# Layer 0's modulation by halves of the features on TensorE, with one strict order of loads

## The chip, the cores and the metric

The kernel runs on one core of a Trainium2 chip. The metric is device time in microseconds (us): the time of one execution of the whole program, of which the profile's span, from the first to the last recorded instruction, is nearly all. The core has a matrix engine (TensorE; PE in the profile, its weight loads PEld), a vector engine (VectorE, DVE), a scalar engine (ScalarE, ACT), a general engine (GpSimd, POOL) and one that only issues transfers and waits (SyncE, SP). Each engine works through its own queue in order. Sixteen DMA engines carry the transfers.

## What is computed

A backbone of two layers over 1024 latent tokens and 256 context tokens with 1024 features. Each layer normalises its tokens, scales and shifts them by a modulation that is worked out from a conditioning vector, and mixes them. Cut to what matters here (layer 0):

```python
def modulation(cond, w, b):
    m = jax.nn.silu(cond) @ w + b
    return jnp.split(m, 3, axis=-1)          # shift, scale, gate

sh_l, sc_l, g_l = modulation(c, mod_w[i], mod_b[i])
sh_c, sc_c, g_c = modulation(c_ctx, mod_w[i], mod_b[i])
h_lat = rms_norm(x_lat, norm_g[i]) * (1.0 + sc_l[:, None, :]) + sh_l[:, None, :]
h_ctx = rms_norm(x_ctx, norm_g[i]) * (1.0 + sc_c) + sh_c
y_lat, y_ctx = even_mixer(h_lat, h_ctx, ev_w_in[j], ...)   # starts with h @ w_in
```

The even mixer projects h to queries, keys, values and gates and runs two kinds of attention (global, and banded with a sink). Layer 1 runs a convolution module and a neighbourhood attention. Everything is float32; a large matmul is made of three with operands split into a high and a low part (`mm3`, L318).

## The kernel before, in words

**Layout.** Tokens lie in the free dimension, features on the 128 partitions: 1024 features are DK = 8 slices called dk. Tokens come in three chunks (`CHUNKS`): chunk 0 is the context (256 tokens), chunks 1 and 2 are 512 latent tokens each. The normalised and modulated tokens are kept as a high and a low part, h[c][0] and h[c][1], of type float32r.

**The modulation.** It has three parts (0 shift, 1 scale, 2 gate) of 1024 features, each worked out in two halves j of 512 features; one half needs 2.1 MB of `mod_w`, in four loads of 512 KB. `mod_half` (L170) does a half on TensorE: eight matmuls (L179) of the two conditioning vectors with 128 x 512 weights, a copy of the row on ScalarE (L181), four small transposes (L184), then the bias on VectorE (L188) and for the scale one more step (L190). `mod_half_v` (L194) does a half on VectorE: per dk and vector one multiply-add of 128 x 512 (L215, L220), then eight small matmuls (L226). The weights' tiles come from a ring (`mw_tile`, L150; `MWR` has six places, two of them in a pool of their own, the others in memory that the attention uses later for keys and values: tags KA, KB, V).

**The start of layer 0** (L623 to 691) is driven by the string `PLAN = 'p0mvnbwmm1h2nbhnbh'`: `0`, `1`, `2` load a chunk (`load_x`), `m` and `v` do the next modulation half on TensorE or VectorE in the order (0,0), (0,1), (1,0), (1,1) (part, j), `n` sums a chunk's squares (`norm_x`, L650), `b` turns that into the reciprocal root, spread over the partitions by small matmuls (`rstd_steps`, L245), `h` makes a chunk's h (`make_h`, L302) and `w` loads and splits the first unit's weights (`load_w0`: eight slices of 128 x 384, 192 KB each, raw tiles `wr` with WRB = 2 buffers). So (0,1) is on VectorE. `make_h` takes, per slice, one VectorE step x * scale * rstd (L307), then either ScalarE's shift into the high part and a VectorE step for the low part (L310, L311), or ScalarE's shift, ScalarE's cast (L297) and a subtraction on POOL (L300). `HV` says which.

**What sets the order.** The code gives priorities; a scheduler orders each engine's queue by a simulated timeline when the program is built, so instructions traced later can come earlier. Two means bind it. `tc.issue_after(ins)` puts the instructions of a block that run on the engine of `ins` behind it in that engine's queue; before, `after_mod(k)` puts the loads of `1`, `2` and `w` behind the last four modulation loads traced ahead of them. `later(n)` lowers priority.

**What comes after.** `proj_qkv` (L760) projects the ten blocks of 128 tokens of a unit of 384 columns: per block eight dk times `mm3`, 24 matmuls of 128 x 384, into a PSUM bank, which ScalarE copies (L773); rotary steps on VectorE and transposes (`qk_tail`) follow, and the results go to DRAM. `proj_gate` (L738) projects the gates. `fill0(0, w0)` (L836) runs this for the first unit (u = 2, as `ORDER` says) before attention starts. While it runs (`solo`), banks of tag "pp" alternate between "pp" and "mx", two buffers each (L104), and every third dk calls `tick()` (L710), which takes one step of `mods`: the remaining eight halves of modulation (layer 0's gate and layer 1), on VectorE at low priority, in tiles of the ring "ABAV" (KA, KB, KA, V). After that `attn_gen` weaves attention groups with the other units' projections; a group starts with a load of keys into a KA tile (`load_ka`, L520).

Of the kernel before, what the change touches and what calls it, by code (L numbers as in the profile page):

```python
# [18 lines left out]
P = 128  # L19
DK = 8  # L20
# [29 lines left out]
PFB = 2  # L50
MWB, WRB = 2, 2
OHQ = 0
# [17 lines left out]
GL = 12  # L70
HV = (('gggvvvvg',) * 3, ('gggvvvvg', 'vvvgvvvg', 'gggvvvvg'))
O1 = (6, 65, 41, 14)
TICK0, TICK1 = (1, 3)
PLAN = 'p0mvnbwmm1h2nbhnbh'
MWR = "ABxAVx"
XA = 4
ORDER = (2, 3, 0, 1)
# [11 lines left out]
def tile_kernel(ctx: ExitStack, tc: tile.TileContext, a, out):  # L89
# [57 lines left out]

    mm0 = []

    def mw_tile():  # L150
# [19 lines left out]
    def mod_half(pool, l, part, j):  # L170

        pb = bank("pp", nm("pm"))
        c0 = part * 1024 + j * 512
        for d2 in range(4):
            w2 = mw_tile()
            mm0.append(SY.dma_start(w2, a["mod_w"][l, 2 * d2 * P : (2 * d2 + 2) * P, c0 : c0 + 512].rearrange("(d p) n -> p d n", d=2)))
            for d in range(2):
                dk = 2 * d2 + d
                PE.matmul(pb[0:2, :], csil[:, dk, :], w2[:, d, :], start=(dk == 0), stop=(dk == DK - 1))  # L179
        row = a0.tile([P, 512], F32, tag="ost", name=nm("mrow"), bufs=2)[0:2, :]  # L180
        SC.copy(row, pb[0:2, :])  # L181
        tr = bank("tr", nm("trm"))
        for i in range(4):
            PE.transpose(tr[:, 2 * i : 2 * i + 2], row[:, i * P : (i + 1) * P], ident[0:2, 0:2])  # L184
        trv = tr[:, 0:8].rearrange("p (i c) -> p i c", c=2)
        o = part * 8 + j * 4
        dst = modT[l][:, o : o + 4, :]
        VE.tensor_tensor(dst, trv, modb[:, l, o : o + 4, None].broadcast_to([P, 4, 2]), op=ALU.add)  # L188
        if part == 1:
            VE.scalar_tensor_tensor(gs[l][:, j * 4 : j * 4 + 4, :], dst, 1.0,  # L190
                                    normg[:, l, j * 4 : j * 4 + 4, None].broadcast_to([P, 4, 2]),
                                    op0=ALU.add, op1=ALU.mult)

    def mod_half_v(pool, l, part, j, conds):  # L194

        c0 = part * 1024 + j * 512
        pool, tag, bufs = (kvp, "QH", 3) if mwp[0] is not None else (pool, "macc", 2)
        accs = [pool.tile([P, 512], F32, tag=tag, name=nm("macc"), bufs=bufs) for _ in conds]
        pre = []
        for dk in range(DK):  # L200
            if solo[0] and dk % 2 == 0:
                w2 = mw_tile()
                d_ = SY.dma_start(w2, a["mod_w"][l, dk * P : (dk + 2) * P, c0 : c0 + 512].rearrange("(d p) n -> p d n", d=2))
                if mwp[0] is not None:
                    mm0.append(d_)
                pre = [w2[:, 0, :], w2[:, 1, :]]
# [28 lines left out]
    def newton_rsqrt(pool, v, n, tag):  # L235
# [7 lines left out]
        return r  # L243

    def rstd_steps(pool, accs, n, tag, inv=1.0, tr="tr"):  # L245
# [12 lines left out]
        yield  # L258
        yield
        bc = bank(tag, nm("bc"))  # L260
        for b in range(nb):
            PE.matmul(bc[:, b * P : (b + 1) * P], r[:, b : b + 1].broadcast_to([P, P]), ident, start=True, stop=True)
        return bc
# [54 lines left out]
    def mm3(o, lh, ll, rh, rl, first, last):  # L318
        PE.matmul(o, lh, rh, start=first, stop=False)  # L319
        PE.matmul(o, lh, rl, start=False, stop=False)  # L320
        done[0] = PE.matmul(o, ll, rh, start=False, stop=last)  # L321

    raws = []

    def load_w(pool, src, c0, nco, width, bufs, leng=lambda dk: "g", dks=range(DK), rb=WPR):

        wh, wl = {}, {}
        for dk in dks:
            raw = pool.tile([P, width], F32, tag="wr", name=nm("wr"), bufs=rb)
            raws.append(SY.dma_start(raw[:, :nco], src[dk * P : (dk + 1) * P, c0 : c0 + nco]))  # L330
            h = pool.tile([P, width], F32R, tag="wh", name=nm("wh"), bufs=bufs)
# [291 lines left out]
    with ExitStack() as p0x:  # L623
        w0p = p0x.enter_context(tc.tile_pool(name="w0p", bufs=1, reuse_waits="tile"))
        W0B = 8

        def load_w0(src, u, n):
            return load_w(w0p, a[src], u * n, n, 384, W0B, rb=WRB)

        with tc.tile_pool(name="st0", bufs=1, reuse_waits="tile") as st0:  # L630
# [4 lines left out]
            def load_x(c):  # L635
# [4 lines left out]
                else:  # L640
                    t = st0.tile([P, DK, n], F32, tag=f"xr{c}", name=f"xr{c}")
                    xraw[c] = [t[:, dk, :] for dk in range(DK)]
                    for d in range(0, DK, 4):
                        SY.dma_start(t[:, d : d + 4, :],
                                     a["cT"][:, d : d + 4, :] if c == 0 else a["xT"][:, d : d + 4, 0:n])
                    return
                for dk in range(DK):
                    SY.dma_start(xraw[c][dk], a["xT"][:, dk, t0 - 256 : t0 - 256 + n])

            def norm_x(c):  # L650
                n = CHUNKS[c][1]
                acc = kvp.tile([P, 512], F32, tag="QH", name=nm("acc"), bufs=3)
                for dk in range(DK):
                    if dk == 0:
                        SC.activation(acc[:, :n], xraw[c][0], AF.Square)
                    else:
                        sq = kvp.tile([P, 512], F32, tag="QL", name=nm("sq"), bufs=3)
                        SC.activation(sq[:, :n], xraw[c][dk], AF.Square)
                        VE.tensor_tensor(acc[:, :n], acc[:, :n], sq[:, :n], op=ALU.add)
                return acc  # L660

            def norm_bc(c, acc):
                n = CHUNKS[c][1]
                return run(rstd_steps(st0, [acc], n, "st"))[:, :n]

            made = [0]
            accs, bcs, mh = [], [], [(0, 0), (0, 1), (1, 0), (1, 1)]
            mwp[0] = st0
            for ev in PLAN:
                if ev in "012":  # L670
                    with after_mod(XA):
                        load_x(int(ev))
                elif ev == "p":
                    SC.dma_start(modb, a["mod_b"])
                    SC.dma_start(normg, a["norm_g"])
                elif ev == "n":
                    accs.append(norm_x(len(accs)))
                elif ev == "w":
                    with after_mod(XA):
                        w0 = load_w0("ev_qkv", ORDER[0], 384)  # L680
                elif ev == "m":
                    mod_half(st0, 0, *mh.pop(0))
                elif ev == "v":
                    run(mod_half_v(st0, 0, *mh.pop(0), (0, 1)))
                elif ev == "b":
                    bcs.append(norm_bc(len(bcs), accs[len(bcs)]))
                elif ev == "h":
                    make_h(0, made[0], lambda dk, c=made[0]: xraw[c][dk], bcs[made[0]], h[made[0]])
                    made[0] += 1

# [904 lines left out]
```

## Time and profile before

| what | value |
|---|---|
| median of three runs | 1595.64 us (1587.97 to 1596.81) |
| the profiled execution | 1590.95 us, span 1589.2 us |
| busy: PE, DVE, POOL, ACT | 1459.0 (92%), 1124.1 (71%), 831.3 (52%), 756.6 (48%) us |
| the chain that ended last, by engine | PE 61%, DVE 15%, DMA 13%, issue 4%, POOL 3%, SPq 2% |
| bytes read from and written to HBM | 160.49 MB, 60.03 MB |

How to read it: busy time is the sum of an engine's instructions, and a busy PE is not PE at its peak, since its matmuls overlap. The profile gives, for stretches of the span, each engine's busy time, the TensorE clock that was granted (1.00 is full speed), the mean busy share of the DMA engines and the bytes moved per time. A timeline row has start, duration, engine, source line, operation, output tile, input tiles and count; square brackets hold the idle time of that engine just before, and what ended it. Line numbers are those of the kernel before; a line can be that of a helper (L300 and L297 are `split`, L319 to L321 `mm3`).

### The profile page before, as it was taken

How to read it: one execution, taken by the hardware profiler on the slowest of the kernel's cores; microseconds unless marked ns; L12 is line 12 of the kernel's file. 1: busy time of each engine (PE TensorE's matmuls, PEld its weight loads, DVE VectorE, ACT ScalarE, POOL GpSimd, SP SyncE). 2: the span in 40 equal slices, each digit the busy share in tenths (PEclk: the TensorE clock that was granted, in tenths of full speed). 3: DMA queues.
4: the chain of work that ended last, by engine and by line, in shares of the span. 5: the costliest groups of instructions: out<-in, count | busy, mean ns of one | idle time of the engine just before them, and what ended most of it. 6: DMA issues, size and time to landing. Idle time of an engine off the chain costs nothing.

```text
span 1589.2 us, 22236 instructions
## 1 busy us (share of the span) xinstructions
PE 1459.0 (92%) x6984; PEld 1180.6 (74%) x6984; DVE 1124.1 (71%) x2172; ACT 756.6 (48%) x1542; POOL 831.3 (52%) x760
## 2 busy tenths in 40 slices
PE   6789989998999988989999889999999999789895
PEld 1779867787778667767887768888887787577685
DVE  4898787588857668455478776999846467576676
ACT  2722353444434664654555564443433455545473
POOL 1561364455636667756654655754532334444575
PEclk9999999998999999989999989999999999799997
DMA  9548234532442123471111122213456878888732
GB/s 316 179 144 270 83 101 138 176 95 80 146 143 75 36 65 113 156 223 51 57 40 44 57 66 79 92 55 107 162 176 219 246 222 262 239 219 232 221 97 106
DMA packets 198462, 222.01 MB, mean 140 GB/s; under 512 B 18812, under 2 KB 154696, under 8 KB 198344
## 3 DMA queue, kind: packets, MB, share of 16 engines
q1 hardware_dynamic: 191680, 209.02, 42.9%
q10 hardware_dynamic: 6664, 11.57, 2.4%
q8 instruction: 55, 0.90, 0.2%
q14 instruction: 63, 0.52, 0.1%
HBM read 160.49 MB, written 60.03 MB: 139 GB/s over the span
## 4 chain that ended last, share of the span: by engine, by line
PE 61%; DVE 15%; DMA 13%; issue 4%; POOL 3%; SPq 2%; ACT 1%; DVEq 0%; POOLq 0%; ACTq 0%
PE p L320 6%; PE p L319 6%; PE p L321 6%; PE ov L411 4%; PE ov L413 4%; PE ov L412 3%; PE po L320 3%; PE po L319 3%; PE po L321 3%; PE st L448 3%; PE st L452 3%; DMA mw<-in_mod_w_dram 3%; DMA QH<-QD 2%; PE pq L321 2%; PE pq L319 2%
## 5 line engine op out<-in xcount | busy, mean ns | idle before, releaser
L300 POOL TENSOR_TENSOR pl<-pf,ph 128x512 fp32r<-128x512 f32 (+4 forms) x321 | 394.1, 1239 | 304.4 <-ACT ph L297 252.4
L300 POOL TENSOR_TENSOR wl<-wr,wh 128x256 fp32r<-128x256 f32 (+2 forms) x256 | 199.3, 794 | 218.2 <-ACT wh L297 209.4
L460 ACT ACTIVATE pf<-st 128x512 f32<-128x512 f32 x284 | 166.2, 596 | 171.3 <-PE st L452 126.5
L297 ACT CAST ph<-pf 128x512 fp32r<-128x512 f32 (+4 forms) x364 | 209.9, 588 | 38.4 <-PE ov L412 22.0
L297 ACT CAST wh<-wr 128x256 fp32r<-128x256 f32 (+2 forms) x264 | 103.4, 404 | 162.4 <-DMA wr<-in_od_d_dram 38.6
L319 PE MATMUL p<-hh,wh 128*128 128x512 f32 x448 | 177.2, 397 | 2.4 <-DVE spk L300 1.4
L320 PE MATMUL p<-hl,wh 128*128 128x512 f32 x448 | 178.4, 399 | 0.4 <-POOL hl L300 0.4
L321 PE MATMUL p<-hh,wl 128*128 128x512 f32 x448 | 173.3, 396 | 0.2 <-POOL wl L300 0.2
L411 PE MATMUL ov<-ph,Vt 128*128 128x512 f32 (+4 forms) x364 | 144.8, 398 | 15.4 <-DVE y L602 8.2
L413 PE MATMUL ov<-pl,Vt 128*128 128x512 f32 (+4 forms) x364 | 144.5, 397 | 7.5 <-POOL pl L300 5.5
L448 PE MATMUL st<-QH,KAt 128*128 128x512 f32 (+4 forms) x364 | 142.5, 393 | 5.4 <-ACT pf L460 3.4
L412 PE MATMUL ov<-ph,Vt 128*64 128x512 f32 (+4 forms) x364 | 142.0, 390 | 0.0
L452 PE MATMUL st<-QL,KBt 68*128 68x512 f32 (+4 forms) x364 | 137.5, 387 | 0.7 <-DVE QL L390 0.7
L1081 DVE SCALAR_TENSOR_TENSOR cps<-U,taps,cps 128x512 f32<-128x512 f32 x184 | 124.3, 747 | 0.0
L565 DVE TENSOR_REDUCE mp<-mx 128x1 f32<-128x512 f32 x128 | 85.9, 683 | 49.7 <-PE mx L564 49.1
L220 DVE SCALAR_TENSOR_TENSOR macc<-mw,csil,macc 128x512 f32<-128x512 f32 x107 | 93.1, 889 | 23.5 <-DMA mw<-in_mod_w_dram 21.4
L319 PEld LDWEIGHTS p<-hh,wh 128*128 128x128 f32 x448 | 84.1, 188 | 23.4 <-DVE spk L300 1.6
L321 PEld LDWEIGHTS p<-hh,wl 128*128 128x128 f32 x448 | 84.4, 189 | 20.5 <-POOL wl L300 0.6
L320 PEld LDWEIGHTS p<-hl,wh 128*128 128x128 f32 x448 | 84.2, 188 | 19.5 <-POOL hl L300 0.8
L411 PEld LDWEIGHTS ov<-ph,Vt 128*128 128x128 f32 x364 | 71.9, 197 | 32.9 <-issue 8.6
L413 PEld LDWEIGHTS ov<-pl,Vt 128*128 128x128 f32 x364 | 71.6, 197 | 31.5 <-POOL pl L300 8.5
L321 PE MATMUL pq<-wh,hl 128*128 128x384 f32 x256 | 88.7, 348 | 1.1 <-DVE hl L311 0.7
(276 smaller groups left out, 3521.5 us busy)
## 6 DMA issues: line engine op xcount, KB each, us to landing
mw<-in_mod_w_dram SPq DMA_DIRECT2D x34, 512.0 KB, 5.6
Q<-qs SPq DMA_DIRECT2D x40, 256.0 KB, 2.7
QH<-Q SPq DMA_DIRECT2D x80, 128.0 KB, 2.8
wr<-in_od_d_dram SPq DMA_DIRECT2D x64, 128.0 KB, 2.9
mw<-in_mod_w_dram SPq DMA_DIRECT2D x28, 256.0 KB, 3.3
wr<-in_ev_qkv_dram SPq DMA_DIRECT2D x32, 192.0 KB, 3.4
KAt<-KD SPq DMA_DIRECT2D x16, 384.0 KB, 6.1
wr<-in_od_wo_dram SPq DMA_DIRECT2D x48, 128.0 KB, 3.0
```

Of the source, the lines that this page charges most:

```text
L297: SC.copy(hi, src)
L300: (GP if leng == "g" else VE).tensor_tensor(lo, src, hi.bitcast(F32), op=ALU.subtract)
L319: PE.matmul(o, lh, rh, start=first, stop=False)
L320: PE.matmul(o, lh, rl, start=False, stop=False)
L321: done[0] = PE.matmul(o, ll, rh, start=False, stop=last)
L411: PE.matmul(o, V[:, 64:192], ph[:, :n], start=(t == 0), stop=False)
L412: PE.matmul(g.ov[0:64, q0 : q0 + n], V[:, 0:64], ph[:, :n], start=False, stop=False)
L413: pvs.append(PE.matmul(o, V[:, 64:192], pl[:, :n], start=False, stop=(last and g.sink is None)))
L448: sts.append(PE.matmul(st[:, :n], KA[:, cs], g.QH[:, q0 : q0 + n], start=True, stop=False))
L452: PE.matmul(st[:, :n], KB[0:68, cs], g.QL[0:68, q0 : q0 + n], start=False, stop=True)
L460: SC.activation(pf[:, :n], st[:, :n], AF.Exp, scale=1.0 if g.bias else SCALE)
L1081: VE.scalar_tensor_tensor(pc, uc, w, pc, op0=ALU.mult, op1=ALU.add)
```

## The change

The plan string, `norm_x`, `norm_bc` and `mod_half_v`'s special case go. The start of layer 0 is written out:

- All four halves of shift and scale go through `mod_half`, on TensorE. The order is by halves of the features: (0,0) and (1,0) first, which give shift and scale for the slices dk 0 to 3 (`front`), and (0,1), (1,1) after chunk 1 and the weights, for dk 4 to 7 (`back`). Odd halves use the PSUM bank "ov".
- Every load of this stage is put behind the one before it on SP (`in_turn`): context, (0,0), (1,0), the first four weight slices, chunk 1, the other four slices, (0,1), (1,1), chunk 2. The ring has eight places (four tiles in the pool of its own rather than two), the raw weight slices four buffers.
- `make_h0` makes h for some slices. With the spread rstd at hand it scales by scale and rstd on VectorE and shifts on ScalarE; for slices that were already multiplied by rstd (`scaled`) it scales and shifts in one VectorE step with two scalars. ScalarE casts the high part, and POOL or VectorE (`HV0`) subtracts for the low part. Chunks 0 and 1 are made in two halves, chunk 2 at once.
- `start_qkv` runs the first unit's projection of the two context blocks for the front slices, 24 matmuls, into two banks that stay open; `proj_qkv` goes on from dk 4 in these. (Those two blocks then call `tick()` twice each and not three times.)
- `behind` puts chunk 1's norm behind the front modulation (TensorE) and chunk 0's front h (ScalarE), the casts of the back weights behind the latter, (0,1)'s matmuls behind the early projection, (1,1)'s behind chunk 1's spread, and chunk 2's norm behind (1,1), chunk 1's front h and chunk 1's scaling.

```diff
-MWB, WRB = 2, 2
+MWB, WRB = 2, 4
+HV0 = ('vvvvgvgv', 'gvgvgvgv', 'gvgvgvgv')
-PLAN = 'p0mvnbwmm1h2nbhnbh'
-MWR = "ABxAVx"
-XA = 4
+MWR = "ABxAVxxx"
...
+    queue = []
+
+    def in_turn(dma):
+
+        with ExitStack() as cx:
+            if queue:
+                cx.enter_context(tc.issue_after(queue[-1].ins))
+            queue.append(dma())
+        return queue[-1]
...
     def mod_half(pool, l, part, j):
-        pb = bank("pp", nm("pm"))
+        pb = bank("ov" if j else "pp", nm("pm"))
...
-            mm0.append(SY.dma_start(w2, ...))
+            mm0.append(in_turn(lambda: SY.dma_start(w2, ...)))
...
+            last = PE.transpose(tr[:, 2 * i : 2 * i + 2], row[:, i * P : (i + 1) * P], ident[0:2, 0:2])
...
+        return last
...
             raw = pool.tile([P, width], F32, tag="wr", name=nm("wr"), bufs=rb)
-            raws.append(SY.dma_start(raw[:, :nco], src[dk * P : (dk + 1) * P, c0 : c0 + nco]))
+            load = lambda: SY.dma_start(raw[:, :nco], src[dk * P : (dk + 1) * P, c0 : c0 + nco])
+            raws.append(in_turn(load) if mwp[0] is not None else load())
...
+            def scaled(c, bc, dks):
+
+                for dk in dks:
+                    last = VE.tensor_tensor(xraw[c][dk], xraw[c][dk], bc, op=ALU.mult)
+                return last
+
+            def make_h0(c, dks, bc=None):
+
+                cond = 1 if c == 0 else 0
+                for dk in dks:
+                    x = xraw[c][dk]
+                    scale, shift = gs[0][:, dk, cond : cond + 1], modT[0][:, dk, cond : cond + 1]
+                    if bc is not None:
+                        VE.scalar_tensor_tensor(x, x, scale, bc, op0=ALU.mult, op1=ALU.mult)
+                        SC.activation(x, x, AF.Identity, bias=shift)
+                    else:
+                        VE.tensor_scalar(x, x, scale, shift, op0=ALU.mult, op1=ALU.add)
+                    hi, lo = h[c][0][:, dk, :], h[c][1][:, dk, :]
+                    last = SC.copy(hi, x)
+                    (GP if HV0[c][dk] == "g" else VE).tensor_tensor(lo, x, hi.bitcast(F32), op=ALU.subtract)
+                return last
+
+            def start_qkv(w):
+
+                wh, wl = w
+                for j in range(2):
+                    begun[j] = bank("pp", nm("pq"))
+                    for dk in front:
+                        last = mm3(begun[j][:, :384], Hs(h, 0, j * P, P, dk), Hs(h, 1, j * P, P, dk), wh[dk], wl[dk],
+                                   dk == 0, False)
+                return last
...
+            front, back = range(0, 4), range(4, DK)
             mwp[0] = st0
-            for ev in PLAN:
...
+            load_x(0)
+            run(mod_half(st0, 0, 0, 0))
+            known = run(mod_half(st0, 0, 1, 0))
+            bc = norm0(0)
+            scaled(0, bc, back)
+            wf = load_w0("ev_qkv", ORDER[0], 384, front)
+            made = make_h0(0, front, bc)
+            load_x(1)
+            pq = start_qkv(wf)
+            with behind(known, made):
+                bc = norm0(1)
+            spread1 = spread[0]
+            with behind(made):
+                wb = load_w0("ev_qkv", ORDER[0], 384, back)
+            w0 = tuple({**f, **b} for f, b in zip(wf, wb))
+            made, ready = make_h0(1, front, bc), scaled(1, bc, back)
+            with behind(pq):
+                run(mod_half(st0, 0, 0, 1))
+            with behind(spread1):
+                known = run(mod_half(st0, 0, 1, 1))
+            make_h0(0, back)
+            load_x(2)
+            make_h0(1, back)
+            with behind(known, made, ready):
+                bc = norm0(2)
+            make_h0(2, range(DK), bc)
...
-                    pp = bank("pp", nm("pq"))
-                    for dk in range(DK):
+                    d0 = 4 if u == ORDER[0] and j in begun else 0
+                    pp = begun[j] if d0 else bank("pp", nm("pq"))
+                    for dk in range(d0, DK):
```

More of the change, by code (lines that the diff above doesn't have):

```diff
@@ L175, in mod_half @@
             w2 = mw_tile()
-            mm0.append(SY.dma_start(w2, a["mod_w"][l, 2 * d2 * P : (2 * d2 + 2) * P, c0 : c0 + 512].rearrange("(d p) n -> p d n", d=2)))
+            mm0.append(in_turn(lambda: SY.dma_start(w2, a["mod_w"][l, 2 * d2 * P : (2 * d2 + 2) * P, c0 : c0 + 512]
+                                                    .rearrange("(d p) n -> p d n", d=2))))
             for d in range(2):
@@ L179, in mod_half @@
                 PE.matmul(pb[0:2, :], csil[:, dk, :], w2[:, d, :], start=(dk == 0), stop=(dk == DK - 1))
+            yield
         row = a0.tile([P, 512], F32, tag="ost", name=nm("mrow"), bufs=2)[0:2, :]
@@ L183, in mod_half @@
         for i in range(4):
-            PE.transpose(tr[:, 2 * i : 2 * i + 2], row[:, i * P : (i + 1) * P], ident[0:2, 0:2])
+            last = PE.transpose(tr[:, 2 * i : 2 * i + 2], row[:, i * P : (i + 1) * P], ident[0:2, 0:2])
         trv = tr[:, 0:8].rearrange("p (i c) -> p i c", c=2)
@@ L192, in mod_half @@
                                     op0=ALU.add, op1=ALU.mult)
+        return last
     def mod_half_v(pool, l, part, j, conds):
         c0 = part * 1024 + j * 512
-        pool, tag, bufs = (kvp, "QH", 3) if mwp[0] is not None else (pool, "macc", 2)
-        accs = [pool.tile([P, 512], F32, tag=tag, name=nm("macc"), bufs=bufs) for _ in conds]
+        accs = [pool.tile([P, 512], F32, tag="macc", name=nm("macc"), bufs=2) for _ in conds]
         pre = []
@@ L202, in mod_half_v @@
                 w2 = mw_tile()
-                d_ = SY.dma_start(w2, a["mod_w"][l, dk * P : (dk + 2) * P, c0 : c0 + 512].rearrange("(d p) n -> p d n", d=2))
-                if mwp[0] is not None:
-                    mm0.append(d_)
+                SY.dma_start(w2, a["mod_w"][l, dk * P : (dk + 2) * P, c0 : c0 + 512].rearrange("(d p) n -> p d n", d=2))
                 pre = [w2[:, 0, :], w2[:, 1, :]]
@@ L243, in newton_rsqrt @@
         return r
+    spread = [None]
     def rstd_steps(pool, accs, n, tag, inv=1.0, tr="tr"):
@@ L261, in rstd_steps @@
         for b in range(nb):
-            PE.matmul(bc[:, b * P : (b + 1) * P], r[:, b : b + 1].broadcast_to([P, P]), ident, start=True, stop=True)
+            spread[0] = PE.matmul(bc[:, b * P : (b + 1) * P], r[:, b : b + 1].broadcast_to([P, P]), ident, start=True,
+                                  stop=True)
         return bc
@@ L321, in mm3 @@
         done[0] = PE.matmul(o, ll, rh, start=False, stop=last)
+        return done[0]
     raws = []
@@ L625, in tile_kernel, with load_w0 @@
         W0B = 8
-        def load_w0(src, u, n):
-            return load_w(w0p, a[src], u * n, n, 384, W0B, rb=WRB)
+        begun = {}
+        def load_w0(src, u, n, dks=range(DK)):
+            return load_w(w0p, a[src], u * n, n, 384, W0B, dks=dks, rb=WRB)
         with tc.tile_pool(name="st0", bufs=1, reuse_waits="tile") as st0:
@@ L643, in load_x, with norm0 @@
                     for d in range(0, DK, 4):
-                        SY.dma_start(t[:, d : d + 4, :],
-                                     a["cT"][:, d : d + 4, :] if c == 0 else a["xT"][:, d : d + 4, 0:n])
+                        in_turn(lambda: SY.dma_start(t[:, d : d + 4, :],
+                                                     a["cT"][:, d : d + 4, :] if c == 0 else a["xT"][:, d : d + 4, 0:n]))
                     return
                 for dk in range(DK):
-                    SY.dma_start(xraw[c][dk], a["xT"][:, dk, t0 - 256 : t0 - 256 + n])
-            def norm_x(c):
+                    in_turn(lambda: SY.dma_start(xraw[c][dk], a["xT"][:, dk, t0 - 256 : t0 - 256 + n]))
+            def norm0(c):
                 n = CHUNKS[c][1]
@@ L659, in norm_x @@
                         VE.tensor_tensor(acc[:, :n], acc[:, :n], sq[:, :n], op=ALU.add)
[L660 to L667, printed above, removed]
-            mwp[0] = st0
-            for ev in PLAN:
[L670 to L689, printed above, removed]
@@ new lines, in norm0 @@
+                return run(rstd_steps(st0, [acc], n, "st", tr="st"))[:, :n]
+            def scaled(c, bc, dks):
[16 more added lines that the diff above has]
+                return last
@@ new lines, in start_qkv, with behind @@
+            def start_qkv(w):
[6 more added lines that the diff above has]
+                return last
+            @contextmanager
+            def behind(*ins):
+                with ExitStack() as cx:
+                    for i in ins:
+                        cx.enter_context(tc.issue_after(i.ins))
+                    yield
@@ new lines, in tile_kernel @@
+            front, back = range(0, 4), range(4, DK)
+            mwp[0] = st0
+            SC.dma_start(modb, a["mod_b"])
+            SC.dma_start(normg, a["norm_g"])
+            load_x(0)
[9 more added lines that the diff above has]
+                bc = norm0(1)
```

## The prediction

> **What bounds the kernel now.** I read the page first, then busy time by stretch, then the timelines of the single engines over the first 170 us, since the change edits nothing behind them but a matmul loop's first index.
>
> ```profile
> span 1589.2 us, 22236 instructions
> ```
> ```profile
> 0.00:46.00 46.00, 27.97 (x84) 7.87 (x84) 23.90 (x49) 15.81 (x35) 8.26 (x14) 0.97 0.92 325
> 46.00:110.00 64.00, 54.73 (x311) 51.83 (x312) 60.08 (x85) 31.97 (x66) 40.75 (x30) 0.95 0.41 132
> 110.00:166.00 56.00, 52.86 (x294) 47.70 (x293) 48.38 (x78) 10.89 (x23) 12.43 (x11) 0.95 0.79 254
> 166.00:1589.00 1423.00, 1323.45 (x6297) 1073.17 (x6297) 991.79 (x1963) 697.96 (x1419) 769.84 (x706) 0.97 0.43 130
> ```
>
> The second fence is busy time by stretch: length, then PE, PEld, DVE, ACT and POOL busy, granted clock, DMA share, GB/s. From 166 us on the TensorE is busy for 1323 of 1423 us, so that long rest is a TensorE queue: what the first stage gains is handed on to it unless something there waits for another date. Of the first 46 us the loads have 92%; from 46 to 110 us the VectorE is busy for 60.1 of 64 us and the TensorE for 54.7. So the first stage is load-bound to 46 us, and after that VectorE and TensorE share the bound. The execution itself took 1590.95 us, its span 1589.2 and 1.75 around it; the three runs have a median of 1595.64 (1587.97 to 1596.81). I work out a gain against 1590.95 and take it off the median. Half a percent, 8 us, is about what a measurement here can tell from no change.
>
> **The first projection, before.** These rows are the TensorE's, start and duration first:
>
> ```profile
> 38.40 1.88 PE L179 MATMUL pm<-mw,csil 128*2 128x512 f32 x4
> 43.72 0.58 PE L184 MATMUL trm<-ident,mrow 2*128 2x2 f32 x4 [3.44 <-ACT mrow L181]
> 46.26 0.69 PE L319 MATMUL pq<-wh,hc 128*128 128x384 f32 x1 [1.96 <-ACT hc L297]
> ...
> 72.89 0.34 PE L319 MATMUL pq<-wh,hh 128*128 128x384 f32 x1
> ...
> 76.36 0.34 PE L321 MATMUL pq<-wh,hl 128*128 128x384 f32 x1
> ```
> ```profile
> 108.24 0.87 ACT L773 COPY pc<-pq 128x384 f32<-128x384 f32 x2
> ```
>
> No projection matmul runs before 46.26 us. The 240 of unit 2 then last until the copy at 108.24: 62.0 us. From 72.89 to 76.36 lie 20 steps, 0.1735 us each, so 240 need 41.6 us and 20.4 us go elsewhere. Three stretches show where:
>
> ```profile
> 56.00:62.00 6.00, 4.02 (x28) 3.76 (x28) 5.05 (x11) 2.04 (x4) 1.78 (x3) 1.00 0.56 166
> 62.00:87.00 25.00, 24.60 (x142) 23.65 (x143) 22.49 (x31) 16.57 (x33) 15.22 (x12) 1.00 0.14 47
> 87.00:110.00 23.00, 16.72 (x99) 15.34 (x98) 22.96 (x26) 5.74 (x13) 16.88 (x12) 0.96 0.46 141
> ```
> ```profile
> 55.24 2.47 POOL L300 TENSOR_TENSOR wl<-wr,wh 128x384 fp32r<-128x384 f32 x2
> ```
>
> TensorE is idle for 2.0 us in 56:62 (the last two weight slices are split only at 55.24 to 57.71, and the second chunk waits for its norm) and for 6.3 us in 87:110 (the VectorE is full there, and chunk 2's low halves come late), while 62:87 is dense. The other 12 us are transposes, norm sums and spreads, and matmuls at a lower clock.
>
> **Part 1: the loads.** The order on SP becomes: context 1.05 MB, modulation (0,0) and (1,0) 2 x 2.10, four slices 0.79, chunk 1 2.10, four slices 0.79, (0,1) and (1,1) 4.19, chunk 2 2.10. The second half of the modulation, without which no group can end, has landed after 13.1 MB.
>
> ```profile
> 25.00:30.00 5.00, 1.00 0.69 240
> 30.00:35.00 5.00, 1.00 0.88 295
> ...
> 45.00:50.00 5.00, 0.50 1.06 387
> ```
>
> Here the last three columns are clock, DMA share and GB/s. A full stretch moves 387 GB/s; 25:35 falls short of it by 1.2 MB, 3 us. At the mean of 325 GB/s of the first 46 us, 13.1 MB take 40.3 us; without the dip, some 37. I take 40, the nearer row being the mean with gaps, since the new order has a gap of its own to risk: the fifth slice waits on SP for a raw buffer that POOL's splitting of the first frees, and behind it in the queue stand three slices, eight modulation loads and chunk 2.
>
> ```profile
> 43.10 0.56 ACT L181 COPY mrow<-pm 2x512 f32<-2x512 f32 x1
> ```
> ```profile
> 46.11 0.17 DVE L190 SCALAR_TENSOR_TENSOR gs<-modT,normg 128x8 f32<-128x8 f32 x1
> ```
>
> A copy of the last modulation's row at 43.10 became a scale at 46.28 (3.2 us), and the last two matmuls take 0.94 (1.88 / 2) ahead of it. So the back half's scale stands at 44.1 at most. A first piece of h then needs a VectorE step, a cast and a split, all in the shadow for later pieces: I take 44.5 for the restart, ends 41 and 47.
> The Trainium skill's page "DMA: Bandwidth & Descriptors", section "Where 436 GB/s comes from", puts the limit of loads from HBM at about 358 GB/s per core. The row with 387 GB/s exceeds it, so the trace decides; by that figure 13.1 MB take 36.6 us behind the first issue, no more than the range above holds.
>
> **Part 2: what is done before the restart.** Modulation (0,1) leaves the VectorE:
>
> ```profile
> L220 DVE SCALAR_TENSOR_TENSOR macc<-mw,csil,macc 128x512 f32<-128x512 f32 x14 | 12.1, 901 | 0.0
> ...
> L659 DVE TENSOR_TENSOR acc<-acc,sq 128x256 f32<-128x256 f32 x7 | 3.6, 518 | 0.0
> ...
> L215 DVE TENSOR_SCALAR macc<-mw,csil 128x512 f32<-128x512 f32 x2 | 0.9, 484 | 4.7 <-DMA mw<-in_mod_w_dram 4.7
> ```
>
> That is 13.0 us off the VectorE, against 8 more matmuls of 128x512 at 0.47 us (1.88 / 4): 3.8 us in a TensorE that waits for loads. It saves nothing by itself while loads bound that time. It makes room: VectorE was busy for 23.9 of the first 46 us, and less these 13.0 it can take the front of chunk 0 and nearly all of chunk 1's norm and scaling. Then 24 of the 240 matmuls (two context banks, features 0 to 511) run in TensorE time that costs nothing: 24 x 0.1735 = 4.2 us off the path, even at the half rate of a clock of 0.50. They hold two of the four alternating banks; the modulation's odd halves move to the "ov" bank, so nobody waits for those. If that cover failed (the first four slices late), the 4.2 us come back.
> On TensorE, (0,1) queues behind these 24 and (1,1) behind chunk 1's spread. I estimate that both waits end before 40 us. The front scale and the first slices are there once 6.0 MB are in (18.5 us at 325 GB/s, plus 3.2), the 24 matmuls by 30; chunk 1 is in after 8.1 MB (25 us), its eight squares and adds at the 0.73 of part 4 by 31, its spread by 37.
> The Trainium skill's "TensorE: Matmul & The Clock Gate", section "What's actually happening", says that an idle window of about 3.4 us halves the clock until about 3.4 us of work. The 0.50 at 45:50 agrees, where the first projections ran. By that rule the early 24 and the restart may each start slow; the first lies off the path and the second is in the 20.4 us already, so the sum keeps its value.
>
> **Part 3: TensorE's sum.** 216 matmuls remain: 37.5 us. Of the 20.4 us I drop the 2.0 of 56:62 (all slices are in by then), 2.0 for chunk 1's norm sums and spread, now ahead, and half of 6.3: 13.2 stay. End 44.5 + 37.5 + 13.2 = 95.2, against 108.2: 13 us. With all 20.4 kept and a restart at 47, the gain is 3; with 10 kept and a restart at 41, 20.
>
> **Part 4: VectorE's sum**, since it is as full. Rows over 46 to 170 us:
>
> ```profile
> L220 DVE SCALAR_TENSOR_TENSOR macc<-mw,csil,macc 128x512 f32<-128x512 f32 x64 | 54.9, 877 | 4.1 <-DMA mw<-in_mod_w_dram 3.3
> L307 DVE SCALAR_TENSOR_TENSOR xr<-xr,gs,bc 128x512 f32<-128x512 f32 (+1 forms) x20 | 12.4, 690 | 3.4 <-PE bc L262 3.4
> L311 DVE SCALAR_TENSOR_TENSOR hl<-xr,modT,hh 128x512 fp32r<-128x512 f32 x8 | 10.0, 1293 | 0.0
> ...
> L659 DVE TENSOR_TENSOR acc<-acc,sq 128x512 f32<-128x512 f32 x9 | 6.4, 725 | 0.3
> ...
> L311 DVE SCALAR_TENSOR_TENSOR hc<-xr,modT,hc 128x256 fp32r<-128x256 f32 x4 | 2.3, 596 | 0.0
> ```
>
> Norms and h took 12.4 + 10.0 + 6.4 + 2.3 = 31.1 us behind 46 us. Behind the restart remain: chunk 2's adds, 7 x 0.73 = 5.1; its eight scalings, 5.5; low halves now as a plain subtraction, two of chunk 0 (0.52 each, the add of 256), two of chunk 1 and four of chunk 2 (0.73): 5.4; and eight scale-and-shift steps with two scalars per partition, a form that is not in the trace. Its nearest row is the tensor-scalar at 0.48 for 512 elements; bounds 0.16 (a small operation, as at 46.11) and 0.73; at 0.48 and half of it for chunk 0, 2.9. Sum 18.9: 12 us less. Two projection groups tick twice rather than three times, so four modulation operations (4 x 0.88 = 3.5 us) fall into the attention, where VectorE has 992 of 1423 us.
>
> **Part 5: where attention starts.**
>
> ```profile
> 158.86 0.50 SPq L522 DMA_DIRECT2D KAt<-K  x1
> ```
> ```profile
> 166.15 1.09 PE L552 MATMUL mx<-KAt,QH 128*128 128x256 f32 x4 [3.29 <-DMA KAt<-K]
> ```
>
> The key tile of the first attention group is one that VectorE's filler modulation uses, so the load at 158.86 waits for VectorE's queue. That date moves by VectorE's 12 to 16 us (with the four operations that fall behind it), TensorE's by 13. I take 13 us. The added buffers (eight modulation tiles for six, four raw slices for two) cost no time of their own; POOL has 10 low halves in h rather than 12. Forecast: 1590.95 - 13 = 1578 for an execution like the profiled one, 1595.64 - 13 = 1582.6 for the median.
>
> **Rivals.** (a) The stalls stay. VectorE's filler is put in its queue by an order fixed when the program is built; if it stands ahead of chunk 2's steps as at 87:110, all 20.4 us are kept: 108.2 - (44.5 + 37.5 + 20.4) = 6 us, 1590, no change. For it: VectorE's 22.96 of 23 us. Against: 12 us less to do.
> (b) The early matmuls do not run early, the order putting them behind the second modulation half: 13 - 4.2 = 9 us, 1587. Against it stands the wait written into (0,1).
> (c) Slower: the one queue. Slices on two raw buffers slipped before:
>
> ```profile
> 32.09 0.50 SPq L330 DMA_DIRECT2D wr<-in_ev_qkv_dram  x1
> 44.61 0.34 SPq L330 DMA_DIRECT2D wr<-in_ev_qkv_dram  x1
> ```
>
> 12.5 us between two slices, while other loads went by. Now nothing may go by: a slip of the fifth slice moves the restart and chunks 1 and 2 with it, one for one. The gain is gone at 13 us, and at 21 the kernel is slower by half a percent; a slip of twice the row, 25 us, gives 1608. Against it: four buffers for four slices, and POOL's 1.2 us a slice (2.47 for two at 55.24), with chunk 1's 2.1 MB, 6 us of loads, to hide behind.
>
> **Numbers.** Forecast 0.57, (b) 0.08, (a) 0.22, (c) 0.13. The forecast and (b), 9 us, are gains over 8: faster 0.65. Same 0.22, slower 0.13. Range: 20 us off the lowest run, 1567, to 1600, which holds (a) and leaves (c) out.
>
> **What would show it.** Right: 24 pq matmuls before 32 us; the last modulation transposes near 42 to 44; pq dense from 45; no macc in the first 40; the last pq copy of unit 2 near 95; KAt issued near 145. Wrong: a wr issue later than 30 us with loads idle behind it; TensorE idle by over 6 us between 65 and 95, waiting for chunk 2's low halves; KAt still at 158, or an early attention whose 1423 us grow by what was won.

## The result, and the profile after

The changed kernel takes 1587.55 us (median of 12 runs, 1577.65 to 1593.47), the kernel before 1597.12 in the same session (12 runs): a ratio of 0.9939, 95% interval 0.9920 to 0.9957. That is 9.6 us, against 13 forecast. Its profiled execution took 1588.68 us, which is only 2.3 less than that of before: single executions differ by more than that (the repeats below), so the profile tells what moved, and the medians tell how much.

The page's head, and busy time by the same stretches as before (length, PE, PEld, DVE, ACT, POOL, clock, DMA share, GB/s; the long rest ends 3 us earlier here):

```profile
span 1586.9 us, 22236 instructions
```
```profile
0.00:46.00 46.00, 32.82 (x106) 13.19 (x107) 17.59 (x44) 17.31 (x39) 11.84 (x17) 0.96 0.97 346
46.00:110.00 64.00, 57.28 (x293) 47.81 (x292) 58.17 (x80) 31.55 (x64) 32.44 (x25) 0.92 0.38 124
110.00:166.00 56.00, 48.76 (x274) 42.77 (x274) 47.26 (x75) 11.94 (x25) 11.55 (x10) 0.97 0.80 238
166.00:1586.00 1420.00, 1323.58 (x6321) 1075.05 (x6321) 998.12 (x1967) 698.53 (x1420) 773.77 (x708) 0.96 0.44 130
```

VectorE has 6.3 us less to do in the first 46 us (17.59 for 23.90), TensorE 4.9 more. From 46 to 110 us, where VectorE was to be relieved, it is as full as before (58.17 for 60.08). The loads gave what was asked of them:

```profile
15.00:20.00 5.00, 5.00 (x16) 1.26 (x15) 1.20 (x4) 1.83 (x4) 0.78 (x1) 1.00 1.06 382
20.00:25.00 5.00, 5.00 (x16) 1.15 (x15) 0.38 (x2) 0.68 (x2) 3.09 (x4) 1.00 1.06 372
25.00:30.00 5.00, 2.12 (x9) 0.98 (x8) 2.41 (x7) 2.40 (x7) 0.00 (x0) 0.94 0.89 294
30.00:35.00 5.00, 5.00 (x23) 5.00 (x22) 3.80 (x6) 5.00 (x13) 1.34 (x2) 0.71 1.04 393
```

One dip, 294 GB/s at 25:30, is left of the old one. But PE is busy for 5.00 of 5.00 us from 15 to 25: TensorE, and not the loads, now sets the pace. By 40 us the stretches of 5 us add up to 13.6 MB, so the 13.1 MB up to the second modulation half were in as forecast. TensorE's timeline (start, duration, line, output, inputs, count) shows with what:

```profile
18.69 5.31 PE L188 MATMUL pm<-mw,csil 128*2 128x512 f32 x12
...
29.43 0.69 PE L330 MATMUL pq<-wh,hc 128*128 128x384 f32 x1 [2.21 <-ACT hc L696]
29.91 0.52 PE L331 MATMUL pq<-wl,hc 128*128 128x384 f32 x1
30.23 0.52 PE L330 MATMUL pq<-wh,hc 128*128 128x384 f32 x1
...
33.19 0.34 PE L330 MATMUL pq<-wh,hc 128*128 128x384 f32 x1
33.36 0.34 PE L331 MATMUL pq<-wl,hc 128*128 128x384 f32 x1
...
35.38 7.03 PE L188 MATMUL pm<-mw,csil 128*2 128x512 f32 x16
...
45.33 1.16 PE L272 MATMUL bc<-ident,nr 128*128 128x128 f32 x8 [1.60 <-DVE nr L250]
46.42 8.72 PE L188 MATMUL pm<-mw,csil 128*2 128x512 f32 x16
55.08 0.44 PE L330 MATMUL pq<-wh,hh 128*128 128x384 f32 x1
...
59.44 0.40 PE L194 MATMUL trm<-ident,mrow 2*128 2x2 f32 x4
61.56 1.05 PE L262 MATMUL trs<-ones,acc 128*128 128x2 f32 x8 [1.72 <-DVE acc L675]
62.53 0.45 PE L330 MATMUL pq<-wh,hc 128*128 128x384 f32 x1
```

A half of the modulation is 16 records of 0.44 us, 7.03 us in all (8.72 where the granted clock was 0.81, from 46 to 55 us), while its 2.1 MB arrive in 5.5 us at 382 GB/s. So the halves pile up on TensorE: (0,1) ends at 42.4, (1,1) waits for chunk 1's spread (45.33 to 46.4) and ends at 55.1, and its transposes stand behind 24 projection matmuls of chunk 1 that are ready first (55.08 to 59.4). The back half's scale is known at 61.43 (the "gs" row of VectorE's timeline), and the projections go on at 62.53, not at 44.5. The last copy of unit 2, on ScalarE, and the first key load on SP:

```profile
112.87 0.86 ACT L832 COPY pc<-pq 128x384 f32<-128x384 f32 x2
```
```profile
158.64 0.50 SPq L535 DMA_DIRECT2D KAt<-K  x1
```

4.6 us later than before, and 0.2 us earlier. The start of the kernel has become no shorter at all. To see where the time went instead, I cut the span at two events that every kernel here has: the first key load, and the first load of layer 1's convolution weights. Before, then after:

```profile
0.00:158.86 158.86, 131.57 (x663) 103.72 (x664) 126.94 (x201) 57.94 (x122) 59.42 (x53) 0.96 0.67 227
158.86:924.13 765.27, 714.37 (x3422) 578.83 (x3420) 526.52 (x1040) 382.14 (x765) 434.56 (x354) 0.97 0.33 98
924.13:1589.20 665.07, 613.08 (x2902) 498.02 (x2901) 470.69 (x933) 316.55 (x656) 337.29 (x353) 0.96 0.56 167
```
```profile
0.00:158.64 158.64, 135.46 (x650) 100.45 (x651) 119.41 (x193) 59.35 (x126) 55.83 (x51) 0.96 0.68 225
158.64:920.66 762.02, 713.80 (x3439) 579.99 (x3437) 528.40 (x1040) 384.14 (x767) 434.15 (x355) 0.97 0.33 98
920.66:1586.90 666.24, 613.18 (x2902) 498.38 (x2901) 473.33 (x933) 315.83 (x656) 339.62 (x353) 0.95 0.56 167
```

In the start TensorE is idle for 23.2 us and not 27.3, and busy for 3.9 more: what was won in waiting went into the modulation half that it took over. VectorE's 7.5 us less there bought nothing, and its waits tell why. What released the first key load last was a step of VectorE's filler modulation (`macc`), in both kernels. Before and after, a row has who waited, for what, the us in total, how often and the longest:

```profile
SPq L522 <- DVE macc L220: 0.5, 1, 0.5
```
```profile
SPq L535 <- DMA K<-qs: 4.3, 1, 4.3
SPq L535 <- DVE macc L228: 0.4, 1, 0.4
```

In the changed kernel that load waited first for the keys to be stored, and then 0.4 us more for the filler. And from 46 us to the key load VectorE is as full after as before:

```profile
46.00:158.86 112.86, 103.59 (x579) 95.86 (x580) 103.04 (x154) 42.13 (x88) 51.16 (x39) 0.95 0.57 187
```
```profile
46.00:158.64 112.64, 102.64 (x547) 87.26 (x546) 101.82 (x149) 42.05 (x87) 43.99 (x34) 0.95 0.56 176
```

Of the 7.5 us, 6.3 were taken off the first 46 us, in which VectorE now waits 7.0 us for the modulation's transposes and 4.3 for chunk 0's spread, both TensorE's. Behind 46 us it has 1.2 us less to do.

This execution wins 3.3 us in the attention of layer 0, whose code the change does not touch (beyond an index), and gives back 1.2 in layer 1.

### The profile page after: what moved, and what is told of

The parts are those of the page before. It is cut to its first block, busy times and chain, and to the rows that moved or that the text cites. A ratio compares the mean times of both kernels' runs of the same rounds, so it can differ in the third digit from the quotient of the medians.

```text
span 1586.9 us, 22236 instructions
## 1 busy us (share of the span) xinstructions
PE 1462.4 (92%) x6988; PEld 1178.8 (74%) x6988; DVE 1121.1 (71%) x2164; ACT 759.3 (48%) x1548; POOL 829.6 (52%) x759
## 5 line engine op out<-in xcount | busy, mean ns | idle before, releaser
L228 DVE SCALAR_TENSOR_TENSOR macc<-mw,csil,macc 128x512 f32<-128x512 f32 x92 | 82.8, 917 | 31.8 <-DMA mw<-in_mod_w_dram 29.2
```

## The experiments

Three theories. **A, the start**: the projections' early start, which the order of loads makes possible, carries the gain. **B, the rest**: the start is as long as before; the gain comes from the queues behind it, which the scheduler lays out anew along its simulated timeline when the start changes. **C, VectorE's relief**: what counts is that (0,1) left VectorE. No kernel here leaves out any of the work.

**Both kernels again**, for the spread between executions of one program.

> The kernel before, once more, for a second trace and the noise. Two theories of where the change gained 0.6% are on trial. A, start-up: the projections of the first unit and the start of attention (the first key load, at 158.86 us before and 158.64 after in the first pair of traces) come earlier by about the gain, and that pair was unlucky. B, the rest: the first stage is as long as it was, and the gain arises behind 166 us. Both expect a ratio of 1.000 (+-0.003) here. A expects the first key load of this trace several us later than in the second trace of the kernel after; B within 2 us of it.

> The kernel after, once more. Both theories: ratio 0.994 (0.991 to 0.997). A: first key load 5 us or more ahead of the repeated kernel before. B: within 2 us, and the loads of the next units' keys (304, 463, 675 us before; 297, 461, 671 after) some 3 to 8 us ahead.

Measured: 1592.86 us, 0.9995 (0.9981 to 1.0009), and 1584.09, 0.9935 (0.9913 to 0.9957). The gain is real and repeats. Before's first key load stood at 158.42 (158.86 the first time), the changed kernel's at 163.80 (158.64):

```profile
0.00:163.80 163.80, 142.73 (x650) 105.60 (x651) 119.70 (x193) 59.10 (x126) 55.54 (x51) 0.92 0.66 218
163.80:921.20 757.40, 710.26 (x3439) 576.23 (x3437) 527.27 (x1040) 383.01 (x767) 434.24 (x355) 0.98 0.33 99
921.20:1583.30 662.10, 610.66 (x2902) 497.56 (x2901) 472.97 (x933) 315.16 (x656) 339.19 (x353) 0.96 0.56 168
```

The changed kernel's first key load came neither 5 us ahead of the other's (A) nor within 2 us of it (B), but 5.4 behind. A start 5 us longer at a clock of 0.92, in an execution that is 3.6 us shorter: in this pair the length of the start does not decide when the end comes.

**Without the wait in front of (1,1).**

```diff
-            with behind(spread1):
-                known = run(mod_half(st0, 0, 1, 1))
+            known = run(mod_half(st0, 0, 1, 1))
```

> The kernel after, with modulation (1,1)'s matmuls no longer put behind chunk 1's spread. In the trace after they stood at 46.4 to 55.1 us and their transposes at 59.4; without the wait they should end near 50 and the back half's projections start near 55 rather than 62.5. A: the first unit's last copy (112.9 us after) and the first key load come some 6 us earlier and the time falls to about 0.990. B: the start moves, the time does not: 0.994.

Measured: 1610.53 us, 1.0099 (1.0075 to 1.0124): 1.6% slower than the changed kernel, which neither theory expected. (1,1) did end earlier, and the projections did not follow. TensorE's timeline:

```profile
43.67 7.03 PE L188 MATMUL pm<-mw,csil 128*2 128x512 f32 x16
50.63 1.16 PE L272 MATMUL bc<-ident,nr 128*128 128x128 f32 x8
51.71 0.41 PE L194 MATMUL trm<-ident,mrow 2*128 2x2 f32 x4
```
```profile
67.12 0.69 PE L332 MATMUL pq<-wh,hc 128*128 128x384 f32 x1 [5.00 <-POOL hc L697]
```

The transposes are 7.7 us earlier (51.71 for 59.44), chunk 1's spread is 5.3 later, and then TensorE stands for 5.0 us for a low half from POOL. So the order of TensorE was not the only limit there. The first key load came at 166.29, 7.7 later, and the attention took 771.9 us; why it took that long is not shown.

**Without the early projection.** `start_qkv` and the first unit's other projections are put behind (1,1)'s transposes; the steps of filler stay the same.

```diff
-            pq = start_qkv(wf)
...
-            with behind(pq):
-                run(mod_half(st0, 0, 0, 1))
+            run(mod_half(st0, 0, 0, 1))
...
+            with behind(known):
+                start_qkv(wf)
+            first = known
...
-        for _ in fill0(0, w0):
-            pass
+        with tc.issue_after(first.ins):
+            for _ in fill0(0, w0):
+                pass
```

> The kernel after, with every projection matmul of the first unit put behind the transposes of modulation (1,1): no early start, all else as after (the same number of ticks). In the trace after, 48 such matmuls ran ahead (24 of the context, 24 of chunk 1), 8.3 us at the warm pitch. A: 4 to 8 us slower than the kernel after, 0.997 to 0.999. B: as the kernel after, 0.994.

Measured: 1579.83 us, 0.9909 (0.9887 to 0.9931). No slower, rather faster than with the early projection (0.9935 in the same session; the intervals overlap). The back half's transposes come at 58.05, the projections start at 58.38, 4.2 earlier than the changed kernel's restart. With 48 more matmuls (8.3 us at 0.1735) to do they end at 115.55, 2.7 later, and the start is 2.0 us longer. Theory A's early start is worth nothing; the attention is shorter all the same:

```profile
0.00:160.64 160.64, 137.55 (x652) 102.01 (x653) 119.54 (x193) 59.40 (x126) 56.14 (x51) 0.95 0.68 222
160.64:915.97 755.33, 708.82 (x3437) 575.25 (x3435) 529.43 (x1040) 385.48 (x767) 435.17 (x355) 0.98 0.33 99
```

**VectorE's relief alone**: the kernel before with (0,1) on TensorE.

```diff
-PLAN = 'p0mvnbwmm1h2nbhnbh'
+PLAN = 'p0mmnbwmm1h2nbhnbh'
```

> The kernel before with one letter of its plan changed: modulation (0,1) on TensorE as well, nothing else. The first theories left two: B, the order of the rest (first stage no shorter, time won or lost behind it because the scheduler lays the queues out anew), and C, VectorE's relief (13 us of multiply-adds off VectorE is what the gain comes from). C: 0.994 or lower, first key load 3 us or more before 158. B: first key load within 3 us of 158, and a ratio that says nothing of VectorE, 0.997 to 1.005 as likely as 0.994.

Measured: 1604.78 us, 1.0075 (1.0046 to 1.0104). VectorE is busy for 114.85 us before the first key load, 12.1 less than before, and yet:

```profile
0.00:161.25 161.25, 134.50 (x635) 100.85 (x635) 114.85 (x184) 57.47 (x120) 56.13 (x52) 0.94 0.68 222
161.25:938.37 777.12, 722.51 (x3453) 584.52 (x3452) 532.50 (x1039) 385.50 (x768) 437.22 (x355) 0.96 0.32 96
```

The start is 2.4 us longer and the attention 11.9. C alone falls: less work on VectorE does not suffice. B's range (0.997 to 1.005) was missed as well.

**Without the strict order of loads**, and **with (0,1) on VectorE in the new start.**

```diff
     def in_turn(dma):
         with ExitStack() as cx:
-            if queue:
-                cx.enter_context(tc.issue_after(queue[-1].ins))
             queue.append(dma())
```

> The kernel after without the strict order: the loads of the start are no longer put behind one another, all else as after. If the strict order carries the gain: 1.000. B and C: the gain does not hang on it, 0.991 to 0.997; the second modulation half is there some us earlier or later as the scheduler places chunk 2.

```diff
+        pool, tag, bufs = (kvp, "QH", 3) if mwp[0] is not None else (pool, "macc", 2)
...
+                    mm0.append(in_turn(load))
...
-            with behind(pq):
-                run(mod_half(st0, 0, 0, 1))
+            run(mod_half_v(st0, 0, 0, 1, (0, 1)))
...
-            with behind(spread1):
-                known = run(mod_half(st0, 0, 1, 1))
+            known = run(mod_half(st0, 0, 1, 1))
```

> The kernel after with modulation (0,1) back on VectorE (16 multiply-adds, 13 us at the prices of the kernel before, at a time when VectorE was busy for 17.6 of 46 us), loads in the same strict order. It takes 7.0 us of matmuls (16 records at 0.43) out of TensorE's queue ahead of (1,1). C: slower than after, back to 1.000. The mis-sized term (a half costs TensorE 7 us and not 3.8): the back half's transposes some 5 us earlier, last copy of unit 2 earlier by as much; the time 0.991 if that reaches the end, 0.994 if the rest decides (B).

Measured: 1585.50 us, 0.9940 (0.9917 to 0.9963), and 1596.02, 1.0011 (0.9988 to 1.0034). The strict order carries nothing that can be measured here. With (0,1) on VectorE the gain is gone, as C has it, but not where C has it. This kernel's stretches, and where TensorE waits in its start:

```profile
0.00:164.54 164.54, 132.49 (x641) 104.75 (x642) 129.91 (x210) 59.24 (x125) 55.01 (x51) 0.91 0.66 217
164.54:918.73 754.19, 709.77 (x3443) 576.46 (x3442) 528.68 (x1040) 384.07 (x766) 434.12 (x356) 0.98 0.34 99
918.73:1591.70 672.97, 614.75 (x2902) 498.01 (x2901) 473.44 (x933) 315.87 (x657) 336.31 (x353) 0.95 0.55 165
```
```profile
47.54 1.87 PE L239 MATMUL trm<-one,macc 128*128 128x2 f32 x8 [12.39 <-DVE macc L233]
```

Its attention, 754.2 us, is the shortest of all; it loses in the start, where TensorE waits 12.39 us for VectorE's rows, and in layer 1. The last transposes of the back half, expected 5 us earlier, come at 66.89, 7.5 later: a half that is dear on TensorE was dearer on VectorE here.

**A nudge**: the changed kernel with eight copies of 16 elements on ScalarE ahead of everything, which leave the order of TensorE's first 230 instructions as it is but for single swaps and move about one in eight behind them.

```diff
+    for _ in range(8):
+        SC.copy(mhalf, mhalf)
```

> The kernel after with eight copies of a 16-element tile on ScalarE (0.2 us each) at the very start, where ScalarE waits for the first load until 5.7 us: they cost nothing themselves. The first 230 or so TensorE instructions keep their order but for single swaps; in the rest about one instruction in eight changes place. C: as after, 0.994. B: the rest decides, so the time may move by 0.3% or more either way with the first key load unmoved.

Measured: 1575.60 us, 0.9877 (0.9847 to 0.9906): work was added, and 0.6%, some 10 us, fell away from the changed kernel. That spoke for B, but the copies stand in the start, which ended 5 us earlier (first key load at 153.57). So the last four runs leave the start alone.

**Order only**: both kernels with another priority for the projections that are woven into layer 0's attention. No operation changes, and TensorE's queue is the same to 200 us at least.

```diff
-FL = (80, -98)
+FL = (78, -98)
```

> The kernel before with FL[0] 78 for 80: layer 0's woven-in projections get a priority two steps earlier. No operation is added, removed or changed, and TensorE's queue is the same for its first 1589 of 6492 instructions (into the second attention unit, near 400 us); behind that about one in eight stands elsewhere. Theory B (the order of the rest decides) expects the first key load at 158 to 159 as before and a total that moves by 0.3 to 1.2 per cent either way, with no cause in the start. Theory A (the start decides; the rest follows at a fixed length) expects a ratio within 0.2 per cent of 1.

> The kernel before with FL[0] 82 for 80. TensorE's queue is the same for its first 855 instructions (near 200 us); behind that one in sixteen stands elsewhere. Theory B: the first key load at 158 to 159, the total moved by 0.2 to 1 per cent either way. If one of this and the run with 78 comes to 0.994 or less, a change of the size of the one studied needs no change of the start at all. Theory A: within 0.2 per cent of 1.

> The changed kernel with FL[0] 79 for 80; the first 919 instructions of TensorE's queue (near 220 us) are the same, one in five behind them stands elsewhere. Theory B: the first key load at 158 to 164 as in the changed kernel, the ratio to the kernel before anywhere from 0.985 to 1.003. If the start itself carried the gain, it would stay at 0.991 to 0.996.

> The changed kernel with FL[0] 82 for 80; the first 918 instructions of TensorE's queue are the same, one in seven behind them stands elsewhere. Theory B: as for 79, a ratio between 0.985 and 1.003, and not the same as that with 79; the start's theory: 0.991 to 0.996.

Measured, before with 78 and 82: 1596.67 us, 1.0010 (0.9987 to 1.0032), and 1590.55, 0.9967 (0.9950 to 0.9984). The changed kernel with 79 and 82: 1582.28, 0.9910 (0.9883 to 0.9938), and 1582.68, 0.9931 (0.9900 to 0.9962). Before with 82, then the changed kernel with 79:

```profile
0.00:159.07 159.07, 133.59 (x646) 104.80 (x647) 126.02 (x200) 57.09 (x121) 58.29 (x53) 0.92 0.69 227
159.07:919.07 760.00, 712.67 (x3439) 579.05 (x3437) 531.42 (x1041) 383.05 (x766) 436.64 (x354) 0.97 0.33 98
```
```profile
0.00:159.00 159.00, 138.31 (x651) 103.58 (x652) 119.15 (x193) 58.95 (x126) 56.59 (x51) 0.94 0.68 225
159.00:916.20 757.20, 709.50 (x3438) 576.30 (x3436) 529.00 (x1040) 386.54 (x767) 435.04 (x355) 0.98 0.33 99
```

In these four runs an order alone is worth 0.1 to 0.3%, not the 0.6% that B needs. With 78 the total did not move by the 0.3% that B expected, with 82 it moved by more than A's 0.2%. The ratios with the old start (without the run that moved (0,1)) run from 0.9967 to 1.0010, those with the new one (its variants that keep (0,1) on TensorE and (1,1)'s wait) from 0.9877 to 0.9940. They don't meet, though the interval of the old start with 82 reaches down to 0.9950 and that of the loose order up to 0.9963. So B in its strong form, that any small edit could have brought this, finds no support here. It is not ruled out: four orders are few, and the nudge, which changed orders both in the start and behind it, was worth 0.6%.

What is left: over four profiled executions with the old start (before, its repeat, 78, 82) and seven with the new one (the changed kernel, its repeat, no early projection, loose order, nudge, 79, 82) the mean span falls by 7.5 us, from 1588.6 to 1581.0 (differences before rounding). The start gives 0.4 of it (158.8 to 158.3), layer 0's attention 4.8 (762.2 to 757.5), layer 1 2.3 (667.6 to 665.2). That is not the whole gain: between the means of the medians lie 11.8 us, since the profiled executions with the old start took 3.9 us less than their medians on the mean, those with the new one 0.3 more. Where the other 4 us lie is in no trace. In the attention TensorE's idle time falls by 3.0 us (49.9 to 46.9) and its busy time, for the same work, by 1.8. Place by place it is a sum of stages won and lost; two stretches of layer 1, before and then after:

```profile
1340.00:1400.00 60.00, 50.48 (x232) 39.93 (x231) 41.95 (x103) 32.78 (x70) 25.64 (x28) 0.86 0.78 231
1220.00:1260.00 40.00, 36.41 (x167) 28.81 (x165) 14.21 (x35) 11.04 (x22) 9.26 (x12) 0.96 0.80 236
```
```profile
1340.00:1400.00 60.00, 56.68 (x289) 46.69 (x288) 43.22 (x97) 34.03 (x76) 27.05 (x28) 0.97 0.86 253
1220.00:1260.00 40.00, 29.31 (x119) 21.72 (x118) 14.76 (x36) 11.15 (x22) 13.45 (x16) 0.79 0.82 230
```

6.2 us of TensorE's waiting gone from the one, 7.1 added to the other. **Open** is whether the new start hands on something that helps, or whether its coarse layout of the rest is merely the better of two: each start has one of its own (matched in sequence behind the first key load, 57% of TensorE's records stand alike in the traces of the two kernels, against 75 to 93% for each kernel and its variants counted here), and no run put the one start before the other's layout. Likeness alone is not enough: without (1,1)'s wait 84% of the order is the changed kernel's, and the attention takes 771.9 us. Nor did a run take the new steps of h (`make_h0`), the added buffers or the two missing ticks alone.

## Why the prediction came near, and where it failed

The forecast was 13 us and 9.6 were measured, but hardly any of it by the way that was forecast: that the size came near is luck.

**The sum of the loads held.** The fifth slice was issued at 20.25 us, the eighth at 25.83, beside the one dip. Rival (c) did not occur.

**The step that failed first is Part 2's price of a modulation half**, "8 matmuls x 0.47 = 3.8 us in a TensorE that waits for loads". The row behind it, 1.88 us for four records, is one load of 512 KB, which holds two of the eight matmuls: TensorE leaves two records for each matmul of this kind, and a half measures 7.03 us. Against 5.5 us of loading it is TensorE that sets the pace, and the loads are in first. Each of the four halves then costs some 1.5 us more than its load, and (0,1) did not fit in free time. The row of the first half in the trace of before, 16 records, would have told it. Part 1's "the last two matmuls take 0.94" has the same slip: they take 1.88.

**The restart (Part 1) failed with it**: 44.5 forecast, 62.53 measured. Of the 18 us, the front half's scale is 5.9 late (27.6, not 18.5 + 3.2 = 21.7), and the rest is what queues on TensorE between the halves: 24 early matmuls that ended at 35.4, not 30; (1,1) behind a spread that ended at 46.4, not 37; and 24 matmuls of chunk 1 that slipped in ahead of (1,1)'s transposes, which I had not priced. The estimate "both waits end before 40 us" was true of the first alone.

**Part 3's sum held from the restart on, by two misses that cancel**: 50.7 us forecast from restart to last copy (37.5 + 13.2), 50.3 measured, but with 24 matmuls fewer (33.3 us for the other 192), so 17.0 us went elsewhere and not 13.2. The end was 112.87, not 95.2, as late as the restart was.

**Part 4 had VectorE's relief too large and in the wrong place.** Behind 46 us the norms and h took 30.0 us, against 31.1 before and 18.9 in the sum. The steps that it priced at 18.9 took 22.5, and 7.5 us more, chunk 1's scalings and its first two low halves, which were to be done before the restart, ran from 46.5 to 53.9. The scale-and-shift step with two scalars was priced at 0.48 for 512 elements and half of it for 256; in VectorE's groups of 46 to 170 us it took 0.88 and 0.52:

```profile
L694 DVE TENSOR_SCALAR xr<-xr,gs,modT 128x512 f32<-128x512 f32 x4 | 3.3, 883 | 0.0
```
```profile
L694 DVE TENSOR_SCALAR xr<-xr,gs,modT 128x256 f32<-128x256 f32 x4 | 1.8, 518 | 0.0
```

What VectorE was spared lay ahead of 46 us, and it waited for TensorE there.

**Part 5 is refuted**: the key load is not near 145 but at 158.64, which the prediction named as a sign against itself. It does wait for VectorE's queue, as Part 5 says, but from 46 us on that queue held 101.8 us of work after 103.0, not 12 to 16 us less. The forecast had 13 us in the start and none behind; in the traces 0.4 of 7.5 us lie in the start. The sentence that failed is "what the first stage gains is handed on": the start gained nothing to hand on. Rival (a), stalls that stay, had the same restart and a start 6 us shorter; the stalls that it named shrank (TensorE's idle time from 87 to 110 us fell from 6.3 to 4.6 us). Rival (b)'s 9 us is the nearest number, again by luck: its early matmuls did run early, and were worth nothing, as their absence showed.

Of the signs, no vector modulation in the first 40 us came true; the 24 early matmuls ran from 29.4 to 35.4, two thirds of them past 32; the transposes, the dense stretch, the last copy and the key load all came 13 to 18 us late. Of the signs against, the key load at 158 came true; TensorE's idle time from 65 to 95 us was 1.9 us, not over 6.

## What to carry to other kernels

Price a moved operation by its own row for the whole of it (16 records, 7.0 us), not by counting source lines times a record, and set it beside the load that it was to hide under. When a scheduler lays out queues, an edit of one stage changes the others: cut every span at events that both kernels have, and ask whether the edited stage became shorter, before believing that the reason held because the time did. Order-only edits (here 0.1 to 0.3% in four runs) give a scale for what the layout alone can make, and a handful of them is few.

## What the runs showed of the hardware

**The granted clock goes with the kernel and with the time.** Its mean over a kernel's timed runs was 0.9592 to 0.9595 for the kernel before (each session's 17 to 26 runs), 0.9599 to 0.9614 for its repeat and its order-only variants, and 0.9641 to 0.9672 for the changed kernel, its repeat and the five variants that kept the gain; the three that lost it had 0.958, 0.960 and 0.960. Between 0.9595 and 0.965 lie 0.6% of TensorE's speed, about as much as the gain. The executions of one program differ in the same sense: over the 17, 17 and 26 of the kernel before, time and clock have a correlation of -0.74, -0.78 and -0.52, with 0.6 to 1.0 us less for 0.001 more clock. By these slopes, an estimate, the clock would go with 3 to 6 us of the gain. But the repeat, the same program in the same session, had 0.9614 where before had 0.9592 and took as long (0.9995). Which is the cause isn't shown: a queue with fewer waits may be granted more. The four rows of layer 1 above go that way: the clock was 0.97 where TensorE was busy for 56.68 of 60 us and 0.86 where for 50.48, 0.96 for 36.41 of 40 and 0.79 for 29.31.

The early projection starts slow: its steps are 0.32 us apart at 29.91 and 0.17 from 33.19 on, 3.8 us after the first. The Trainium skill's "TensorE: Matmul & The Clock Gate", section "What's actually happening", has about 3.4 us of work before the clock doubles, and the trace agrees.

One and the same program differed by 5 us in its start (158.64 and 163.80 us to the first key load, at a clock of 0.96 and 0.92), and in the other direction by 4.6 and 4.1 in the two stretches behind it.
